# A hybrid attention step on one core: rests of the weights in pieces, the sample's search ended later and with a running count, the last output tile in halves

## Chip, cores and metric

The kernel runs on one core of one Trainium2 chip. The metric is the device time of one execution in microseconds; the median of 3 runs of the kernel before is 369.21 us (368.37 to 370.45).

## What is computed

One inference step of one layer, for a prompt of 512 tokens and a sample of 32 tokens, width 1024, all in float32:

```python
z = _rmsnorm(x, g) @ w_in
oa = _band_prompt(qa, ka, va, rel_bias_a)      # group A: 6 heads x 64, own chunk and 8 before it
ob = _dsa_prompt(qb, kb, vb, qi, ki, wi)       # group B: only the top-k keys of an indexer's scores
om = _attend(qm, mk, mv, None)                 # group M: 4 heads over 256 memory tokens
o = concat([oa * silu(ga), ob * silu(gb), om * silu(gm)])
y = _rmsnorm(x + o @ w_out, g_final)
```

The sample does the same against caches; its group B chooses 256 of 1056 keys per query (`lax.top_k`, which takes the earlier key where two scores are equal). The new keys and values of all groups are outputs too.

## The kernel before

Each float32 product is made of three fp32r products. A weight chunk `raw` is rounded by ScalarE to `wh`; its rest `wl = raw - wh` is made in one subtraction by GpSimd, for chunks 0 and 2 by VectorE (`w_split`, lines 429 to 445). The tokens are split in the same way into `xTh` and `xTl`, and TensorE adds `xTh*wh`, `xTl*wh` and `xTh*wl`. A chunk holds 4, 2 or 3 blocks of 128 rows and 128 to 384 columns.

The Python code is also the planner. `Line` keeps a clock for every engine with its own costs; work beside the projections is written as generators, which wait with `yield` until a time or with `line.wait` until a condition. `line.run` gives out the matmuls of a projection one after the other, and ahead of each it lets every generator run whose time has come (`beside`). The order in which the instructions are given out is the order on each engine, so a different condition or cost at one place reorders the others after it. All instructions are made through helpers, so the profile puts them on one line (L240), and they are known by the tiles that they write and read.

The order of projections is the indexer's (`i`), then `EARLY` (group A, memory, their queries and gates), then `LATE`: `gb0`, `kb`, `qb`, `vb`, `gb1`, `gb2`. Meanwhile the indexer's scores are made, VectorE picks the prompt's keys (`picks`, MAX8 and MATCH_REPLACE8 on `ysel`), and attention units (`attend`) follow one another: scores into two PSUM banks (`bank<-k,q`), VectorE reads them, ScalarE takes the exponent, TensorE turns the result (`ident,z`) and multiplies by the values (`pt,v`), and `finish` multiplies by the gate (`o<-bank,gate`), which frees the bank. There are eight PSUM banks.

Rows of kb and qb pass through `rope` (line 718): two products out of PSUM (`rt`, `kb` or `qb`) and a sum by VectorE or GpSimd. There is one tile `rt`, so the next rope waits for the sum before it.

`sample_rows` (line 470) collects the sample's own rows of each projection (`kaS`, `kbS`, `qbS`, ...), scales them and applies rope. `sample_choice` (line 942) finds the 256th largest score of each sample query: 16 rounds, each two ScalarE passes over 1056 keys, a matmul of one column (`bank<-bf_ok,over`) and some VectorE instructions of one element. Its end finds the exact threshold `t` and then, in six more rounds of the same kind over `rank`, the position `cut` up to which keys equal to `t` are taken. The mask is left in `ysS` for `sample_b`.

At the end `out_part` multiplies by `w_out` in column groups (256 wide for groups A and M, 512 wide for B as two halves in one bank); for each token tile `evict` adds the bank to `xr` and `settle` makes the final norm: Square with a sum on ScalarE, the sum and the power on GpSimd, two halves of the row scaled by VectorE and ScalarE, and the store by SyncE's queue.

Of the kernel before, what the change touches and what calls it, by code (L numbers as in the profile page):

```python
# [9 lines left out]
F32 = mybir.dt.float32  # L10
# [3 lines left out]
ALU = mybir.AluOpType  # L14
# [3 lines left out]
P = 128  # L18
# [251 lines left out]
def hybrid_step(ctx: ExitStack, tc: tile.TileContext, a: dict):  # L270
# [25 lines left out]
    def give(*tiles):  # L296
        free_banks.extend(held.pop(t.tensor.name) for t in tiles)
# [131 lines left out]
    def w_split():  # L429
        at = {}  # L430
        for i in range(len(w_list)):
            far = i >= n_in + 3 and i % 2
            yield from line.wait(lambda: len(raws) > i and (not far or wq))
            pw, n = (rp, 4) if i < 4 else (wq[0], 2) if far else (wp, 3)
            mine = at.setdefault(n, [])
            yield from line.wait(lambda: len(mine) < n or used["done"] > mine[-n])
            mine.append(i)
            raw = raws[i]
            yield max(line.at(raw), pw.free("wl"))
            wh = pw.tile(list(raw.shape), F32R, tag="wh", name="wh", bufs=n)  # L440
            wl = pw.tile(list(raw.shape), F32R, tag="wl", name="wl", bufs=n)
            rounded(wh, raw)
            yield line.at(wh) - 0.2
            tsub(V if i in WV else G, wl, raw, f(wh))
            split.append((wh, wl))
# [24 lines left out]
    def sample_rows(nm, n, p):  # L470
# [14 lines left out]
        give(p)  # L485
        yield from line.wait(lambda: NT in normed)
        yield max(line.at(rs[0:T, NT:NT + 1]), line.at(out) - 0.2)
# [449 lines left out]
    bi = {n: cp.tile([P, 1], I32, name="bi_" + n) for n in ("thr0", "thr1", "flip", "neg", "ok", "dig", "next")}  # L937
    bf = {n: cp.tile([P, 1], F32, name="bf_" + n) for n in ("sum", "t", "c", "m", "need", "cut", "try", "dig", "min")}
    bf["ok"] = cp.tile([P, 1], BF16, name="bf_ok")
    over4 = cp.tile([P, 4, T], BF16, name="over4")  # L940

    def sample_choice():
        flp, neg, ok, dig, nxt = (bi[n] for n in ("flip", "neg", "ok", "dig", "next"))
        thr = bi["thr0"], bi["thr1"]
        s_, t, c, m, need, cut, tr_, digf, okf = (bf[n] for n in ("sum", "t", "c", "m", "need", "cut", "try", "dig", "ok"))
# [4 lines left out]
        V.tensor_copy(digf, dig)  # L950
        G.memset(over4, 0.0)
# [3 lines left out]

        def passed(of, bias, least_, scale=1.0):

            yield line.at(bias)
            A.activation(junkS, of, AF.Sign, bias=bias, accum_out=s_)
            A.activation(okf, s_, AF.Sign, bias=least_, scale=scale)  # L960
# [15 lines left out]
        for b in range(30, -1, -2):  # L976
# [561 lines left out]
    projections(LATE)  # L1538
    line.until(lambda: 1 in gated and all(n in over for n in ("kb", "qb", "vb")))
    rox.close()  # L1540
# [36 lines left out]

    def out_part(parts, c0, n, done, order):

        ws = [w_next(1 + i) for i in range(len(parts))]  # L1580
        for t in order:
            acc, = take(1)
            for i, ((m, k0, nk, p0, pn), (wh, wl)) in enumerate(zip(parts, ws)):
                o = acc[:, p0:p0 + pn]
                yield (wh, wl) + ((acc,) if i == 0 else ()) + ((oS[:, k0:k0 + nk, :],) if t == NT else
                                  tuple(x[:, :, t * P:(t + 1) * P] for x in oT[m]))
                for k in range(nk):
# [6 lines left out]
                    else:  # L1594
# [4 lines left out]
                        PE.matmul(o, hh, wl[:, k, :], start=False, stop=en)  # L1599
            line.spawn(evict([acc], [1], lambda _, p, t=t: residual(t, p, c0, n), lambda t=t: done(t)))  # L1600

# [5 lines left out]
    for c0 in range(0, D, 256):  # L1607
        line.run(out_part(((0, 0, 3, 0, 256), (2, 6, 2, 0, 256)), c0, 256, lambda t: None, (0, 1, 2, 3, NT)))
    line.until(lambda: 1 in over and count["done"] == len(units))
# [8 lines left out]

    def settle(t, c0):
        rows = P if t < NT else T  # L1620
        x = xr[t][:, c0:c0 + 512]
        s_ = ss[:rows, t, :]
        last = c0 + 512 == D
        yield line.at(x) - 0.2
        A.activation(sq[:rows], x, AF.Square, scale=D ** -0.5, accum_out=s_[:, c0 // 512:c0 // 512 + 1])
        if not last:
            G.tensor_tensor(x, x, gf[:rows, c0:c0 + 512], op=ALU.mult)
        yield line.at(s_) - 0.2
        if not last:
            V.tensor_scalar(s_[:, 2:3], s_[:, 0:1], EPS, None, op0=ALU.add)  # L1630
# [12 lines left out]
    while line.tasks:
# [66 lines left out]
```

## Time and profile before

| | us |
|---|---|
| median of 3 runs | 369.21 |
| time of the profiled execution | 369.7 |
| its span (first to last instruction) | 367.9 |
| TensorE busy | 355.6 (97%) |
| VectorE busy | 282.4 (77%) |
| ScalarE busy | 223.0 (61%) |
| GpSimd busy | 176.2 (48%) |

The profile is of one execution. PE is TensorE, PEld its weight loads, DVE VectorE, ACT ScalarE, POOL GpSimd, SP SyncE. A row of the timeline gives start, duration, engine, operation, output and inputs, how many, and in brackets the idle time of the engine ahead of it and what ended it. 1.8 us of the execution lie outside the span.

### The profile page before, as it was taken

To read this page: it belongs to the slowest core of one execution; us is meant where nothing else is said; L and a number is where in the kernel's file an instruction comes from. 1 tells how busy PE (TensorE), PEld (TensorE's weight loads), DVE (VectorE), ACT (ScalarE), POOL (GpSimd) and SP (SyncE) were. 2 spreads that over 40 slices of the span, in tenths; PEclk is the share of its full clock that TensorE was granted. 3 is DMA by queue.
4 is the path that set the end of the run, shared out by engine and by line. 5 is a ranking of instruction groups with operands and counts; after the bars stand their busy time and mean duration, and the time that the engine had idled before them with its cause. 6 is when DMAs were issued, how large, how long until landed. Compare 5 with 4: busy or idle time off the path is not lost.

```text
span 367.9 us, 7969 instructions
## 1 busy us (share of the span) xinstructions
PE 355.6 (97%) x2959; PEld 321.6 (87%) x2959; DVE 282.4 (77%) x731; ACT 223.0 (61%) x524; POOL 176.2 (48%) x202
## 2 busy tenths in 40 slices
PE   8999999999999999999999998999999999999992
PEld 8989679999989988889899787898999879899991
DVE  2682996989999999999999989986764676623553
ACT  5865756997776946788737343767864556311343
POOL 1787953475443834446548447352145206233651
PEclk9999999999999999999999998999999999999998
DMA  7996631366483330611322115121147932120005
GB/s 252 361 361 220 172 116 43 130 178 172 127 272 104 116 89 11 175 47 45 86 64 67 45 48 172 37 59 54 48 159 259 375 98 88 43 102 2 0 20 224
DMA packets 41478, 46.35 MB, mean 126 GB/s; under 512 B 5184, under 2 KB 36544, under 8 KB 41440
## 3 DMA queue, kind: packets, MB, share of 16 engines
q1 hardware_dynamic: 41440, 45.85, 39.2%
q8 instruction: 23, 0.38, 0.4%
q14 instruction: 15, 0.12, 0.1%
HBM read 39.67 MB, written 6.16 MB: 125 GB/s over the span
## 4 chain that ended last, share of the span: by engine, by line
PE 77%; DVE 11%; ACT 3%; POOL 3%; issue 2%; DMA 2%; SPq 1%; POOLq 0%; ACTq 0%; DVEq 0%
PE bank L240 77%; DMA raw<-in_w_in_dram 2%; DVE rt L240 1%; POOL wl L240 1%; DVE rank L240 1%; DVE KSs L240 1%; ACT sq L240 1%; DVE ysel L240 1%; DVE kb L240 1%; POOL ss L240 1%; DVE kbS L240 1%; DVE m L240 1%; SPq L240 1%; DVE bf_m L240 1%; POOL kb L240 1%
## 5 line engine op out<-in xcount | busy, mean ns | idle before, releaser
L240 POOL TENSOR_TENSOR wl<-raw,wh 128x512 fp32r<-128x512 f32 (+2 forms) x68 | 105.1, 1553 | 95.6 <-ACT wh L240 91.8
L240 PE MATMUL bank<-wh,xTh 128*128 128x384 f32 (+1 forms) x192 | 67.5, 351 | 0.1
L240 ACT ACTIVATE wh<-raw 128x512 fp32r<-128x512 f32 (+2 forms) x70 | 49.8, 717 | 28.4 <-issue 11.8
L240 PE MATMUL bank<-wl,xTh 128*128 128x384 f32 (+1 forms) x192 | 64.0, 334 | 0.2 <-DVE wl L240 0.2
L240 PE MATMUL bank<-wh,xTl 128*128 128x384 f32 (+1 forms) x192 | 63.7, 332 | 0.0
L240 ACT ACTIVATE z<-z,st 128x256 f32<-128x256 f32 (+3 forms) x76 | 40.6, 549 | 35.1 <-DVE st L240 35.0
L240 PE MATMUL bank<-xTh,wh 128*128 128x272 f32 x208 | 46.3, 304 | 0.3 <-DVE stS L240 0.3
L240 PE MATMUL bank<-xTh,wl 128*128 128x272 f32 x208 | 43.0, 288 | 0.0
L240 PE MATMUL bank<-xTl,wh 128*128 128x272 f32 x208 | 43.0, 288 | 0.0
L240 PEld LDWEIGHTS bank<-wh,xTh 128*128 128x128 f32 x192 | 36.6, 191 | 3.9 <-issue 2.6
L240 PEld LDWEIGHTS bank<-wl,xTh 128*128 128x128 f32 x192 | 36.5, 190 | 0.6 <-DVE wl L240 0.4
L240 PEld LDWEIGHTS bank<-wh,xTl 128*128 128x128 f32 x192 | 36.8, 191 | 0.3 <-DVE xTl L240 0.3
L240 PEld LDWEIGHTS bank<-xTh,wh 128*128 128x128 f32 x208 | 32.7, 189 | 3.1 <-issue 2.0
L240 PEld LDWEIGHTS bank<-xTl,wh 128*128 128x128 f32 x208 | 32.6, 188 | 0.0
L240 PEld LDWEIGHTS bank<-xTh,wl 128*128 128x128 f32 x208 | 32.5, 189 | 0.0
L240 DVE MAX8 m<-ysel 128x8 f32<-128x256 f32 (+2 forms) x48 | 26.4, 550 | 0.1
L240 DVE MATCH_REPLACE8 ysel<-m,ysel 128x256 f32<-128x256 f32 (+2 forms) x48 | 26.0, 542 | 0.0
L240 PE MATMUL bank<-ident,z 128*128 128x128 f32 (+1 forms) x161 | 25.2, 274 | 0.5 <-ACT z L240 0.4
L240 DVE TENSOR_TENSOR xr<-bank,xr 128x256 f32<-128x256 f32 (+1 forms) x24 | 12.2, 510 | 16.7 <-PE bank L240 15.6
L240 PEld LDWEIGHTS bank<-ident,z 128*128 128x128 f32 (+1 forms) x161 | 18.3, 140 | 3.6 <-issue 1.4
L240 DVE SCALAR_TENSOR_TENSOR ysel<-r,wI,ysel 128x256 f32<-128x256 f32 (+2 forms) x21 | 18.5, 880 | 3.0 <-ACT r L240 2.5
L240 ACT ACTIVATE junkS<-ysS,bi_neg 128x1056 int8<-128x1056 f32 x16 | 18.7, 1172 | 2.3 <-DVE bi_neg L240 2.3
(317 smaller groups left out, 884.1 us busy)
## 6 DMA issues: line engine op xcount, KB each, us to landing
raw<-in_w_in_dram SPq DMA_DIRECT2D x20, 384.0 KB, 3.3
raw<-in_w_in_dram SPq DMA_DIRECT2D x26, 256.0 KB, 2.9
raw<-in_w_out_dram SPq DMA_DIRECT2D x8, 384.0 KB, 3.0
nat<-in_x_prompt_dram SPq DMA_DIRECT2D x4, 512.0 KB, 8.2
raw<-in_w_mem_kv_dram SPq DMA_DIRECT2D x8, 256.0 KB, 2.9
xr<-in_x_prompt_dram SPq DMA_DIRECT2D x4, 512.0 KB, 5.3
out_dram<-xr SPq DMA_DIRECT2D x4, 512.0 KB, 2.6
xr<-in_x_t_dram SPq DMA_DIRECT2D x3, 544.0 KB, 5.9
```

The costliest lines, as they stand in the source:

```text
L240: return fn(*args, **kw)
```

## The change

Five edits, in the order of the code:

1. `w_split`: the rest `wl` is made in two instructions (chunks of 4 or 2 blocks) or three (3 blocks) in place of one.
2. `sample_rows`: the rows kbS and qbS are scaled and turned by rope only when the prompt's qb is finished.
3. `sample_choice`: the end of the search waits for that too. The six rounds for `cut` go; in their place stand a mask of keys equal to `t` (int8), a running count over it (`tensor_tensor_scan`) and one comparison with the number that is still needed.
4. `out_part`: in the last column group the last prompt tile (`apart`) uses two banks, each added to `xr` and squared by itself; `settle` takes pieces of any width.
5. `settle`: the left half of the prompt's third tile is scaled by VectorE in place of ScalarE.

```diff
@@ w_split
-            tsub(V if i in WV else G, wl, raw, f(wh))
+            step = max(raw.shape[1] // 2, 1)
+            for k in range(0, raw.shape[1], step):
+                c = slice(k, k + step)
+                tsub(V if i in WV else G, wl[:, c], raw[:, c], f(wh)[:, c])
@@ sample_rows
-        yield from line.wait(lambda: NT in normed)
+        yield from line.wait(lambda: NT in normed and (nm not in ("kb", "qb") or "qb" in over))
@@ sample_choice
-        yield from line.wait(lambda: count["scored"] >= len(TILES))
+        yield from line.wait(lambda: count["scored"] >= len(TILES) and "qb" in over)
...
         V.tensor_scalar(junkS, ysS, t, None, op0=ALU.is_gt, op1=ALU.add, accum_out=c)
-        V.tensor_scalar(need, c, -2.0, float(2 * TOPK_S - NKS) + 0.5, op0=ALU.mult, op1=ALU.add)
-        G.iota(rank, pattern=[[-1, NKS]], base=2048, channel_multiplier=0, allow_small_or_imprecise_dtypes=True)
-        yield max(line.at(rank), line.idle(V))
-        V.scalar_tensor_tensor(rank, ysS, t, rank, op0=ALU.is_equal, op1=ALU.mult)
-        V.memset(cut, 2048.5)
-        V.tensor_scalar(tr_, digf, 1024.0, cut, op0=ALU.mult, op1=ALU.subtract)
-        for b in range(10, -1, -2):
-            w = float(1 << b)
-            p = yield from passed(rank, tr_, need, -1.0)
-            V.tensor_scalar(m, p[:, 0:1], 0.5 * w, 1.5 * w, op0=ALU.mult, op1=ALU.add)
-            give(p)
-            V.tensor_scalar(cut, m, -1.0, cut, op0=ALU.mult, op1=ALU.add)
-            if b:
-                V.tensor_scalar(tr_, digf, 0.25 * w, cut, op0=ALU.mult, op1=ALU.subtract)
+        V.tensor_scalar(need, c, -1.0, TOPK_S + 0.5, op0=ALU.mult, op1=ALU.add)
+        V.tensor_scalar(junkS, ysS, t, None, op0=ALU.is_equal)
+        yield line.idle(V)
+        V.tensor_tensor_scan(rank, junkS, junkS, 0.0, op0=ALU.add, op1=ALU.max)
+        yield line.idle(V)
+        V.scalar_tensor_tensor(rank, rank, need, junkS, op0=ALU.is_lt, op1=ALU.mult)
         yield line.idle(V)
         V.tensor_scalar(ysS, ysS, t, BIG, op0=ALU.is_le, op1=ALU.mult)
         yield line.idle(V)
-        V.scalar_tensor_tensor(ysS, rank, cut, ysS, op0=ALU.is_le, op1=ALU.mult)
+        V.scalar_tensor_tensor(ysS, rank, 0.5, ysS, op0=ALU.is_lt, op1=ALU.mult)
@@ out_part
+                if i and t in apart:
+                    line.spawn(evict([acc], [1], lambda _, p, t=t: residual(t, p[:, 0:p0], c0, p0),
+                                     lambda t=t: done(t, c0, p0)))
+                    acc, = take(1)
@@ settle
-        A.activation(y[:, 0:512], y[:, 0:512], AF.Copy, scale=s_[:, 4:5])
+        V.scalar_tensor_tensor(y[:rows, 512:D], y[:rows, 512:D], run, gf[:rows, 512:D], op0=ALU.mult, op1=ALU.mult)
+        if t == NT - 2:
+            V.tensor_scalar(y[:rows, 0:512], y[:rows, 0:512], run, None, op0=ALU.mult)
+        else:
+            A.activation(y[:rows, 0:512], y[:rows, 0:512], AF.Copy, scale=run)
```

How this moves the instructions is shown at two places, both on VectorE (DVE). The first is ahead of the first read of group B's scores, `z,st<-bank,mb`, which frees the banks of that unit. ISA stands for the fused add with minimum and for the readout of its accumulator; `bf_` and `bi_` are one-element tiles of the search. Before:

```order
L240 TENSOR_TENSOR vbS<-bank,vbS 32x384 x2
L240 COPY pt<-bank 128x512
L240 TENSOR_TENSOR kl<-bank,k 128x512
L240 TENSOR_SCALAR vbS<-vbS,rs 32x384
L240 SCALAR_TENSOR_TENSOR o<-bank,gate 128x256
L240 COPY pt<-bank 128x512
L240 SCALAR_TENSOR_TENSOR ql<-bank,q 128x512
L240 TENSOR_SCALAR bf_m<-bank 128x1
L240 TENSOR_SCALAR bf_cut<-bf_m,bf_cut 128x1
L240 TENSOR_SCALAR bf_try<-bf_dig,bf_cut 128x1
L240 SCALAR_TENSOR_TENSOR o<-bank,gate 128x256
L240 ISA z,st<-bank,mb_68 128x128
```

With the change:

```order
L240 SCALAR_TENSOR_TENSOR ql<-bank,q 128x512
L240 TENSOR_SCALAR rank<-ysS,bf_t 128x528
L240 ISA rank,bf_try<-rank,ysS 128x528
L240 ISA bf_try 128x1
L240 TENSOR_TENSOR bf_m<-bf_m,bf_try 128x1
L240 TENSOR_SCALAR bf_c<-bf_c 128x1
L240 SCALAR_TENSOR_TENSOR bf_m<-bf_c,bf_m 128x1
L240 TENSOR_TENSOR bf_t<-bf_t,bf_m 128x1
L240 TENSOR_SCALAR junkS,bf_c<-ysS,bf_t 128x1056
L240 TENSOR_SCALAR bf_need<-bf_c 128x1
L240 TENSOR_SCALAR junkS<-ysS,bf_t 128x1056
L240 ISA z,st<-bank,mb_68 128x128
```

The second half of the search for the exact threshold, which stood 91 DVE rows ahead of that read before, now lies between the query's low part (`ql`) and the read of the scores. Ahead of `ql` stand, since the last rope of qb, also the first half of that search, the first count, and the ropes of kbS and qbS.

The second place is the end of the program, from the second prompt tile's sum on (`xr_3894`, `xr_3895`, `xr_3896` are the second, third and fourth prompt tile before; `xr_3910`, `xr_3911`, `xr_3912` the same with the change). Before:

```order
L240 TENSOR_TENSOR xr_3895<-bank,xr_3895 128x512
L240 SCALAR_TENSOR_TENSOR xr_3894<-xr_3894,ss,gf 128x512
L240 TENSOR_TENSOR xr_3896<-bank,xr_3896 128x512
L240 SCALAR_TENSOR_TENSOR xr_3895<-xr_3895,ss,gf 128x512
L240 SCALAR_TENSOR_TENSOR xr_3896<-xr_3896,ss,gf 128x512
```

With the change:

```order
L240 TENSOR_TENSOR xr_3911<-bank,xr_3911 128x512
L240 SCALAR_TENSOR_TENSOR xr_3910<-xr_3910,ss,gf 128x512
L240 TENSOR_TENSOR xr_3912<-bank,xr_3912 128x256 x2
L240 SCALAR_TENSOR_TENSOR xr_3911<-xr_3911,ss,gf 128x512
L240 TENSOR_SCALAR xr_3911<-xr_3911,ss 128x512
L240 TENSOR_SCALAR ss<-ss 128x1
L240 SCALAR_TENSOR_TENSOR xr_3912<-xr_3912,ss,gf 128x512
```

The last tile's sum comes in two pieces, the third tile's left half has moved to DVE, and a one-element sum of the last tile's squares (`ss<-ss`) now stands behind both instructions of the third tile.

## Rows read from the trace of the kernel before

**Rows 1.** The page's part 1: busy us, share of the span, instructions.
```profile
PE 355.6 (97%) x2959; PEld 321.6 (87%) x2959; DVE 282.4 (77%) x731; ACT 223.0 (61%) x524; POOL 176.2 (48%) x202
```
**Rows 2.** Waits of PE: who waited for whom, us, times, longest.
```profile
PE bank L240 <- DVE o L240: 1.3, 1, 1.3
PE bank L240 <- DVE stk L240: 0.7, 2, 0.4
```
**Rows 3.** Timeline around PE's longest wait inside the program.
```profile
220.82 3.93 POOL L240 TENSOR_TENSOR wl<-raw,wh 128x768 fp32r<-128x768 f32 x2
...
221.25 1.83 DVE L240 TENSOR_TENSOR kb<-rt,kb 128x384 f32<-128x384 f32 x1
...
222.48 0.38 PE L240 MATMUL bank<-k,q 64*128 64x256 f32 x1
...
223.69 0.42 DVE L240 SCALAR_TENSOR_TENSOR o<-bank,gate 128x256 f32<-128x256 f32 x1
...
224.17 0.38 PE L240 MATMUL bank<-k,q 64*128 64x256 f32 x1 [1.31 <-DVE o L240]
...
225.08 0.44 PE L240 MATMUL bank<-wh,xTh 128*128 128x384 f32 x1
```
**Rows 4.** Groups of DVE by form: busy us, mean ns.
```profile
L240 DVE TENSOR_TENSOR rt<-bank,sin 128x384 f32<-128x384 f32 x8 | 4.4, 553 | 1.8 <-POOL kb L240 1.1 <-POOL qb L240 0.6
...
L240 DVE TENSOR_SCALAR z<-z,st 128x512 f32<-128x512 f32 x6 | 3.2, 531 | 0.2
...
L240 DVE CUSTOM_DVE_ANT_0 rank<-rank,ysS 128x528 f32<-128x528 f32 x2 | 1.9, 937 | 0.1
...
L240 DVE TENSOR_SCALAR_CACHE_REDUCE junkS<-ysS,bf_t 128x1056 int8<-128x1056 f32 x2 | 2.6, 1310 | 0.0
...
L240 DVE SCALAR_TENSOR_TENSOR ysS<-rank,bf_cut,ysS 128x1056 f32<-128x1056 f32 x1 | 1.3, 1318 | 0.0
...
L240 DVE TENSOR_SCALAR bf_try<-bf_dig,bf_cut 128x1 f32<-128x1 f32 x6 | 1.3, 215 | 0.4
```
**Rows 5.** Windows: length, busy us per engine, PE's granted clock, DMA share, GB/s.
```profile
224.00:229.00 5.00, 4.83 (x25) 4.26 (x27) 4.69 (x13) 2.72 (x5) 3.24 (x3) 0.66 0.98 315
```
**Rows 6.** Groups of POOL by form: busy us, mean ns; idle before.
```profile
L240 POOL TENSOR_TENSOR wl<-raw,wh 128x768 fp32r<-128x768 f32 x28 | 51.9, 1861 | 32.6 <-ACT wh L240 31.8 <-POOL keysB L240 0.5
L240 POOL TENSOR_TENSOR wl<-raw,wh 128x512 fp32r<-128x512 f32 x38 | 50.1, 1324 | 57.3 <-ACT wh L240 54.2 <-PE bank L240 2.9
...
L240 POOL TENSOR_TENSOR kb<-rt,kb 128x384 f32<-128x384 f32 x3 | 3.1, 1018 | 5.3 <-DVE kb L240 5.3
...
L240 POOL TENSOR_TENSOR oMl<-o,oMh 128x256 fp32r<-128x256 f32 x4 | 3.0, 739 | 3.9 <-ACT oMh L240 3.9
```
**Rows 7.** Timeline of PE around one matmul of the search's end.
```profile
241.62 0.34 PE L240 MATMUL bank<-wh,xTl 128*128 128x384 f32 x1
241.80 0.34 PE L240 MATMUL bank<-wl,xTh 128*128 128x384 f32 x1
241.98 0.18 PE L240 MATMUL bank<-bf_ok,over 128*128 128x1 bf16 x1
...
242.28 0.34 PE L240 MATMUL bank<-wh,xTl 128*128 128x384 f32 x1
```
**Rows 8.** Timeline of the end: POOL, DVE and ACT after the last matmuls.
```profile
360.62 0.55 POOL L240 TENSOR_TENSOR ss<-ss,nhalf 128x1 f32<-128x1 f32 x1
360.65 0.69 DVE L240 TENSOR_TENSOR xr<-bank,xr 128x512 f32<-128x512 f32 x1 [0.81 <-PE bank L240]
361.20 0.72 ACT L240 ACTIVATE xr<-xr,ss 128x512 f32<-128x512 f32 x1 [0.94 <-POOL ss L240]
361.26 0.74 DVE L240 SCALAR_TENSOR_TENSOR xr<-xr,ss,gf 128x512 f32<-128x512 f32 x1
361.83 0.61 ACT L240 ACTIVATE sq<-xr 128x512 f32<-128x512 f32 x1
...
362.61 0.19 POOL L240 TENSOR_TENSOR ss<-ss 128x1 f32<-128x1 f32 x1 [1.45 <-ACT sq L240]
```

More of the change, by code (lines that the diff above doesn't have):

```diff
@@ L937, in hybrid_step @@
     bi = {n: cp.tile([P, 1], I32, name="bi_" + n) for n in ("thr0", "thr1", "flip", "neg", "ok", "dig", "next")}
-    bf = {n: cp.tile([P, 1], F32, name="bf_" + n) for n in ("sum", "t", "c", "m", "need", "cut", "try", "dig", "min")}
+    bf = {n: cp.tile([P, 1], F32, name="bf_" + n) for n in ("sum", "t", "c", "m", "need", "try", "min")}
     bf["ok"] = cp.tile([P, 1], BF16, name="bf_ok")
@@ L944, in sample_choice @@
         thr = bi["thr0"], bi["thr1"]
-        s_, t, c, m, need, cut, tr_, digf, okf = (bf[n] for n in ("sum", "t", "c", "m", "need", "cut", "try", "dig", "ok"))
+        s_, t, c, m, need, tr_, okf = (bf[n] for n in ("sum", "t", "c", "m", "need", "try", "ok"))
         G.iota(dig, pattern=[[0, 1]], base=0, channel_multiplier=1)
@@ L949, in sample_choice @@
         V.memset(dig[0:T], 1)
-        V.tensor_copy(digf, dig)
         G.memset(over4, 0.0)
@@ L954, in sample_choice, with passed @@
         V.memset(bf["min"], float(NKS - 2 * TOPK_S) + 0.5)
-        def passed(of, bias, least_, scale=1.0):
+        def passed(of, bias, least_):
             yield line.at(bias)
             A.activation(junkS, of, AF.Sign, bias=bias, accum_out=s_)
-            A.activation(okf, s_, AF.Sign, bias=least_, scale=scale)
+            A.activation(okf, s_, AF.Sign, bias=least_)
             yield line.sure(okf)
@@ L1538, in hybrid_step @@
     projections(LATE)
-    line.until(lambda: 1 in gated and all(n in over for n in ("kb", "qb", "vb")))
+    line.until(lambda: 1 in gated and all(n in over and n in news for n in ("kb", "qb", "vb")))
     rox.close()
@@ L1576, in hybrid_step, with out_part @@
     line.spawn(sample_b())
-    def out_part(parts, c0, n, done, order):
+    def out_part(parts, c0, n, done, order, apart=()):
         ws = [w_next(1 + i) for i in range(len(parts))]
@@ L1599, in out_part @@
                         PE.matmul(o, hh, wl[:, k, :], start=False, stop=en)
-            line.spawn(evict([acc], [1], lambda _, p, t=t: residual(t, p, c0, n), lambda t=t: done(t)))
+            f0 = parts[-1][3] if t in apart else 0
+            line.spawn(evict([acc], [1], lambda _, p, t=t, f0=f0: residual(t, p[:, f0:n], c0 + f0, n - f0),
+                             lambda t=t, f0=f0: done(t, c0 + f0, n - f0)))
     def residual(t, acc, c0, n):
@@ L1607, in hybrid_step @@
     for c0 in range(0, D, 256):
-        line.run(out_part(((0, 0, 3, 0, 256), (2, 6, 2, 0, 256)), c0, 256, lambda t: None, (0, 1, 2, 3, NT)))
+        line.run(out_part(((0, 0, 3, 0, 256), (2, 6, 2, 0, 256)), c0, 256, lambda *_: None, (0, 1, 2, 3, NT)))
     line.until(lambda: 1 in over and count["done"] == len(units))
@@ L1617, in hybrid_step, with settle @@
     ss = fp.tile([P, NT + 1, 8], F32, name="ss")
-    def settle(t, c0):
+    pieces = [0] * (NT + 1)
+    def settle(t, c0, n):
         rows = P if t < NT else T
-        x = xr[t][:, c0:c0 + 512]
+        x = xr[t][:, c0:c0 + n]
         s_ = ss[:rows, t, :]
-        last = c0 + 512 == D
+        j = pieces[t]
+        pieces[t] += 1
+        new, run, old = s_[:, 2 * j:2 * j + 1], s_[:, 2 * j + 1:2 * j + 2], s_[:, 2 * j - 1:2 * j]
         yield line.at(x) - 0.2
[L1625 to L1630, printed above, removed]
+        A.activation(sq[:rows, 0:n], x, AF.Square, scale=D ** -0.5, accum_out=new)
+        if j == 0:
+            G.tensor_tensor(x, x, gf[:rows, c0:c0 + n], op=ALU.mult)
+        yield line.at(new) - 0.2
+        if c0 + n < D:
+            V.tensor_scalar(run, new, EPS if j == 0 else old, None, op0=ALU.add)
@@ L1631, in settle @@
             return
-        G.tensor_tensor(s_[:, 3:4], s_[:, 1:2], s_[:, 2:3], op=ALU.add)
-        G.tensor_tensor(s_[:, 4:5], s_[:, 3:4], nhalf[:rows], op=ALU.pow)
-        yield line.at(s_) - 0.2
+        G.tensor_tensor(run, new, old, op=ALU.add)
+        G.tensor_tensor(run, run, nhalf[:rows], op=ALU.pow)
+        yield line.at(run) - 0.2
         y = xr[t]
-        V.scalar_tensor_tensor(x, x, s_[:, 4:5], gf[:rows, c0:D], op0=ALU.mult, op1=ALU.mult)
-        A.activation(y[:, 0:512], y[:, 0:512], AF.Copy, scale=s_[:, 4:5])
+        V.scalar_tensor_tensor(y[:rows, 512:D], y[:rows, 512:D], run, gf[:rows, 512:D], op0=ALU.mult, op1=ALU.mult)
@@ L1638, in settle @@
+        if t == NT - 2:
+            V.tensor_scalar(y[:rows, 0:512], y[:rows, 0:512], run, None, op0=ALU.mult)
+        else:
+            A.activation(y[:rows, 0:512], y[:rows, 0:512], AF.Copy, scale=run)
         DMA.dma_start(a["y_prompt"][t * P:(t + 1) * P, :] if t < NT else a["y_sample"], y)
     for c0 in range(0, D, 512):
-        line.run(out_part(((1, 3, 3, 0, 256), (1, 3, 3, 256, 256)), c0, 512, lambda t, c0=c0: line.spawn(settle(t, c0)),
-                          (NT, 0, 1, 2, 3)))
+        line.run(out_part(((1, 3, 3, 0, 256), (1, 3, 3, 256, 256)), c0, 512, lambda t, c, n: line.spawn(settle(t, c, n)),
+                          (NT, 0, 1, 2, 3), (NT - 1,) if c0 else ()))
```

## Prediction

> **What bounds the kernel now.** I read the page's busy shares first. TensorE is busy for 355.6 of 367.9 us, 97%; no other engine is above 77% [rows 1]. So the time moves only by what is taken from TensorE's own work, from the few places where it stands still, from its clock, or from the end, where it has nothing left to do. A faster GpSimd or VectorE pays only at such a place. I then asked the waits for these places. There is one wait inside the program of more than half a microsecond: 1.3 us on VectorE's `o`, the gate product that frees a bank [rows 2]. The two on `stk` make 0.7 together [rows 2].
>
> The timeline around the long wait tells why `o` is late. GpSimd makes rests of 128x768, two in 3.93 us [rows 3]. At 221.25, beside them, VectorE's rope sum `kb<-rt,kb` takes 1.83 us [rows 3], where VectorE's other rope instructions of 128x384 take 0.553 [rows 4]. Its `o` starts only at 223.69 and lasts 0.42; TensorE's next scores start at 224.17 after 1.31 us of nothing [rows 3]. From the windows I read what the pause does afterwards: from 224 to 229 the granted clock is 0.66 on the mean, with TensorE busy for 4.83 of 5.00 us [rows 5]. [...] The pause thus cost 1.3 + 1.7 = 3.0 us.
>
> [...]
>
> **The change, part by part**
>
> *A, the stall at 222.8, −3.0.* The planner gives out a new order, in which the scores that waited here stand earlier, and VectorE no longer turns kbS and qbS nor searches for the sample's threshold near them. If the same meeting occurs, a piece of 384 columns holds VectorE for about 1.02 us (GpSimd's sum of that width) in place of 1.86 [rows 6]. I take the whole 3.0; its bounds are 0 (the pause turns up elsewhere) and −3.0.
>
> *B, the six rounds, −0.7.* Each had a one-column matmul on TensorE. From 241.80 to 242.28 there are two steps with it, 0.48 us; without it one step is 241.80 − 241.62 = 0.18 [rows 7], so 0.48 − 0.36 = 0.12 is its price, six times 0.7. As bounds I take 0.08 and 0.2 each, −0.5 to −1.2. The twelve ScalarE passes and the small instructions of VectorE in these rounds lie beside TensorE's work and bring nothing by themselves.
>
> *C, the end, 0.* The last matmul ends near 360.62. Before, the last tile was added to `xr` at 360.65 in 0.69, its Square was held until 361.83 by ScalarE's scaling of the third tile (361.20, 0.72), and GpSimd's sum stood at 362.61 [rows 8]. Halves free the bank sooner and the scaling leaves ScalarE. But the one-element sum of the last tile's squares now stands on VectorE behind both instructions of the third tile. These can't start before GpSimd's power of that tile ends (360.62 + 0.55 = 361.17): 361.26 + 0.74 [rows 8] + 0.53 for the new scaling (a 128x512 product by a column takes 0.531 [rows 4]) is 362.53, and with the sum itself 362.6 to 362.7, where it was 362.61. So nothing; the bound is −0.9 if that sum doesn't wait, +0.1 if it all follows in a row.
>
> *D, the start, −0.4.* The two `stk` waits make 0.7 [rows 2] and follow VectorE instructions that lie beside long rests. Shorter pieces may take half; bounds −0.7 and +0.7.
>
> *E, a new queue ahead of group B's first scores, +0.8.* This is the place that the first order rows show. After the last rope of qb VectorE has, up to the reads that free the bank for the first matmul of `gb1`: two counts 2 × 1.31, two half searches of a compare (0.69, the price of a 128x512 sum [rows 8]) and a custom operation (0.94), so 2 × 1.63; eight scalings and ropes of kbS and qbS at 0.553 at most; `kl` and `ql` at 0.69 each; nine one-element instructions at 0.215; the int8 mask at 1.31 at most [rows 4]; three score reads at 0.42 (as `o` [rows 3]). That is 2.6 + 3.3 + 4.4 + 1.4 + 1.9 + 1.3 + 1.3 = 16.2 us. TensorE has from the end of qb 96 matmuls at 0.175 (16.8), eight transposes (about 0.9) and the 24 score matmuls (2.5 times the columns that took from 224.17 to 225.08 [rows 3], 2.3), in all 20.0 us. VectorE starts later than that, since the four ropes go one by one through one `rt` tile: two products (1.1) and a sum of 1.02 by GpSimd [rows 6] each, 7.0 for the chain, of which 3.2 lie before the end of qb. So TensorE has 20.0 − 3.8 = 16.2. The two are level: no cover is left. Of the eight instructions with two SBUF inputs (six of the ropes, two of the searches) each can meet a GpSimd piece. I take one such meeting, 1.0, less 0.2 for the scalings and the mask, which I priced at their most. Bounds 0 and, with half of them held for 1.02, +4.
>
> *F, GpSimd's pieces, 0.* A rest of 128x512 as two pieces of 256 costs 2 × 0.739 = 1.48 in place of 1.32; 128x768 as two costs 2.04 in place of 1.86, as three of 256 2.2 [rows 6]. Over 66 rests this is 38 × 0.16 + 28 × 0.2 to 0.36, 12 to 16 us more. GpSimd is busy for 48% [rows 1], and stands idle for 32.6 and 57.3 us ahead of these very instructions, waiting for ScalarE's `wh` [rows 6]: that is the cover. Without it a rest comes up to 0.36 us later.
>
> *G, the running count, 0.* No row of before has a scan. The nearest are the one-pass instructions over 1056 columns, 1.31 and 1.32 [rows 4]; I bound it by one and by two of them, 1.3 and 2.6, and take 2.2. The scan, a comparison and a last product stand behind the first score reads, where the six rounds stood before; what is held there is the next pair's `kl` and `ql`, off TensorE's path by the count of E's kind. [...]
>
> *Sum:* −3.0 − 0.7 + 0 − 0.4 + 0.8 = −3.3. The profiled execution took 369.7 (span 367.9 and 1.8 around it), so 366.4; it stood 0.5 above the median, so **365.9**.
>
> **Rivals**
>
> 1. *Slower: E decides.* Seven of the eight two-input instructions meet GpSimd's pieces, which are now twice as many. TensorE then waits 7 × 1.02 = 7.1 us ahead of `gb1` and, as after the pause of 1.31, loses 1.7 to the clock. With E's 0.8 taken out, the other terms give −4.1; −4.1 + 7.1 + 1.7 is +4.7, **373.9**. With the clock's loss the sign turns at a wait of 2.4, and over 0.5% is lost from 4.3. For it: no slack, the single-file queue. Against: most instructions on VectorE beside rests keep their usual time now, the rope of 1.83 is the exception. Chance 0.12.
> 2. *No change: the pause only moves.* Another bank is freed late by a reordered VectorE, for 1.3 us and 1.7 of clock; B and D and E remain: −0.7 − 0.4 + 0.8 = −0.3, **368.9**. For it: a planner with a new order has many such places, and VectorE is at 77%. Chance 0.25.
> 3. *More is gained.* E costs nothing, the `stk` waits go (−0.7), the last sum isn't held (−0.9): −3.0 − 0.7 − 0.9 − 0.7 = −5.3, **363.9**. This is also where the end's edit does what it appears to be for; my forecast says that it does not. Chance 0.14.
>
> My own case has the rest, 0.49, from 364.2 (no wait in E) to 367.3.
>
> **How the numbers follow.** The measurement can tell about 0.5% from no change, 1.85 us: faster means 367.36 or less, slower 371.06 or more. Faster are my own case and rival 3, 0.63; same is rival 2, 0.25; slower is rival 1, 0.12. The range runs from 362.8 (rival 3 with B at its bound of −1.2 and another half microsecond) to 369.6 (rival 2 with D at its bad end, +0.7), and leaves out rival 1 and a little of both ends, under 0.2.
>
> **What would show it.** A: no wait of TensorE over 1 us on VectorE's `o`, and no stretch of 5 us with a granted clock near 0.66. B: the one-column matmuls fall from 22 to 16. C: GpSimd's last sum about 2.0 us after the last matmul; at 1.2 it is rival 3. D: `stk` below 0.7. E: a wait ahead of the first `gb1` matmul on VectorE's `st`, under 1 us in my case, over 2.4 in rival 1. F: no more than some tenths of waits on `wl`. G: the scan at 1.3 to 2.6 us. The forecast is wrong if the pause, with its clock, is still there in another place, or if the wait in E passes 3 us.

## The result and the profile after

The changed kernel takes 366.24 us (median of 20 runs, 365.49 to 369.11); the kernel before took 369.48 beside it (20 runs). The ratio is 0.9922, with a 95% interval from 0.9908 to 0.9935. The forecast of 365.9 lies close to it, but only in part for its own reasons: as the sections below show, its term E was too kind, its term A counted a loss of the clock that only some runs have, and a gain of about 1.6 us was in no term at all.

The page's busy shares of the changed kernel, in the form of [rows 1]:

```profile
PE 351.2 (96%) x2953; PEld 318.6 (87%) x2953; DVE 270.8 (74%) x710; ACT 216.7 (59%) x514; POOL 197.4 (54%) x278
```

TensorE is still the bound. It is busy for 4.4 us less; GpSimd has 76 instructions and 21.2 us more, of which little is seen on TensorE (its waits on `wl`, the rests that GpSimd makes, are 0.2). TensorE's waits in the changed kernel, which answer to [rows 2]:

```profile
PE bank L240 <- DVE ql L240: 1.6, 1, 1.6
...
PE bank L240 <- ACT wh L240: 0.5, 1, 0.5
PE bank L240 <- DVE st L240: 0.4, 1, 0.4
PE bank L240 <- DVE gate L240: 0.4, 1, 0.4
...
PE bank L240 <- POOL wl L240: 0.2, 1, 0.2
```

The wait on `o` of 1.3 us is gone, and so are the two on `stk`. In their place stands one of 1.6 on `ql`, with 0.4 on `st` behind it. Apart from one of 1.4 on `nhalf` at the start, which both kernels have, the listed waits add up to 3.3 us before and 4.0 after: in sum TensorE does not wait less. The windows around the new wait (length, busy us of the engines, granted clock, DMA share, GB/s), beside [rows 5]:

```profile
252.00:254.00 2.00, 0.36 (x5) 0.20 (x4) 1.97 (x5) 0.58 (x1) 0.76 (x1) 1.00 0.56 166
254.00:259.00 5.00, 4.56 (x35) 3.79 (x35) 4.79 (x20) 0.80 (x5) 0.00 (x0) 1.00 0.19 63
```

The granted clock is 1.00 after this pause of 1.6 us, though it is longer than the one of 1.3 before, after which its mean was 0.66 [rows 5]. Why `ql` is late is seen in the timeline of VectorE from the last ropes of qb on:

```profile
241.00 0.55 DVE L240 TENSOR_TENSOR qb<-bank,cos 128x384 f32<-128x384 f32 x1
241.46 0.14 DVE L240 TENSOR_SCALAR bf_t<-bi_thr 128x1 f32<-128x1 f32 x1
241.64 1.01 DVE L240 SCALAR_TENSOR_TENSOR bf_m<-bf_t 128x1 f32<-128x1 f32 x1
242.69 0.94 DVE L240 SCALAR_TENSOR_TENSOR bf_t<-bf_m,bf_t 128x1 f32<-128x1 f32 x1
243.66 1.32 DVE L240 TENSOR_SCALAR_CACHE_REDUCE junkS<-ysS,bf_t 128x1056 int8<-128x1056 f32 x1
...
244.90 0.87 DVE L240 TENSOR_SCALAR kbS<-kbS,rs 32x384 f32<-32x384 f32 x1
245.88 1.18 DVE L240 TENSOR_TENSOR rt<-kbS,sin64S 32x384 f32<-32x384 f32 x1
247.10 0.98 DVE L240 TENSOR_TENSOR kbS<-kbS,cos64S 32x384 f32<-32x384 f32 x1
248.11 0.98 DVE L240 TENSOR_TENSOR kbS<-rt,kbS 32x384 f32<-32x384 f32 x1
249.02 0.40 DVE L240 TENSOR_SCALAR qbS<-qbS,rs 32x384 f32<-32x384 f32 x1
249.45 0.55 DVE L240 TENSOR_TENSOR rt<-qbS,sin64S 32x384 f32<-32x384 f32 x1
...
252.20 1.12 DVE L240 CUSTOM_DVE_ANT_0 rank<-rank,ysS 128x528 f32<-128x528 f32 x1
253.25 0.68 DVE L240 SCALAR_TENSOR_TENSOR ql<-bank,q 128x512 fp32r<-128x512 f32 x1
```

and in GpSimd's timeline beside it:

```profile
241.62 1.01 POOL L240 TENSOR_TENSOR qb<-rt,qb 128x384 f32<-128x384 f32 x1 [1.14 <-DVE bf_t L240]
242.59 6.09 POOL L240 TENSOR_TENSOR wl<-raw,wh 128x384 fp32r<-128x384 f32 x6
```

While GpSimd works through its rope sum and six pieces in a row, six of the VectorE instructions shown from 241.64 to 248.11, which read SBUF alone, each take about as long as one piece (6.09 / 6 = 1.02): one-element ones 1.01 and 0.94, the rows of kbS 0.87 to 1.18. The count at 243.66 does not: its 1.32 is what it takes in [rows 4]. As soon as the pieces end, at 248.7, the same instructions on qbS take 0.40 and 0.55. I call an instruction that is made longer in this way held, and each such case a meeting. The six held rows add up to 5.96 us; at 0.16, 0.16, 0.40 and three times 0.55 they would be 2.37, so 3.6 us of them are holding. The custom operation at 252.20, beside the next two pieces, is a seventh: 1.12, where the same at 254.37 takes 0.71. In all 4.0 us of VectorE's queue ahead of `ql` are holding.

The end of the program, beside [rows 8], from GpSimd and VectorE:

```profile
357.13 0.55 POOL L240 TENSOR_TENSOR ss<-ss,nhalf 128x1 f32<-128x1 f32 x1
...
357.71 0.75 DVE L240 SCALAR_TENSOR_TENSOR xr<-xr,ss,gf 128x512 f32<-128x512 f32 x1 [0.60 <-POOL ss L240]
358.38 0.48 DVE L240 TENSOR_SCALAR xr<-xr,ss 128x512 f32<-128x512 f32 x1
358.78 0.21 DVE L240 TENSOR_SCALAR ss<-ss 128x1 f32<-128x1 f32 x1
...
359.13 0.19 POOL L240 TENSOR_TENSOR ss<-ss 128x1 f32<-128x1 f32 x1 [1.45 <-DVE ss L240]
```

The last matmul ends at 356.66, so GpSimd's last sum starts 2.47 us after it; before it was 1.99. It waits for VectorE's one-element `ss`, which stands behind the two products of the third tile, as the second order of the change shows.

One more difference is in no wait. At the end of the output projection the matmuls follow each other without a gap in both kernels. The two ends of the last 24 steps, of the kernel before:

```profile
357.46 0.28 PE L240 MATMUL bank<-wl,oBh 128*128 128x256 f32 x1
...
360.34 0.28 PE L240 MATMUL bank<-wl,oBh 128*128 128x256 f32 x1
```

and of the changed kernel:

```profile
353.66 0.28 PE L240 MATMUL bank<-wl,oBh 128*128 128x256 f32 x1
...
356.38 0.28 PE L240 MATMUL bank<-wl,oBh 128*128 128x256 f32 x1
```

24 steps, from start to start, take 2.88 us before (120 ns each) and 2.72 after (113 ns), with a granted clock of 1.00 in both. The output projection has 384 matmuls of this width, so about 2.5 us. The instructions are the same; the tiles are not where they were. The change drops two one-element tiles (`cut` and `dig`), each of which takes 32 bytes of each partition, and the tiles allocated behind them move down by 64 bytes: the addresses of `wh` and `wl`, and of `xTh` and `xTl`, go from 96 to 32 modulo 128. The attention outputs that `wh` and `wl` are multiplied with, `oAh`, `oBh` and `oMh`, stay at 96.

### The profile page after: what moved, and what is told of

It is laid out like the page before. It is cut to its first block, busy times and chain, and to the rows that moved or that the text cites. A ratio compares the mean times of both kernels' runs of the same rounds, so it can differ in the third digit from the quotient of the medians.

```text
span 364.4 us, 8024 instructions
## 1 busy us (share of the span) xinstructions
PE 351.2 (96%) x2953; PEld 318.6 (87%) x2953; DVE 270.8 (74%) x710; ACT 216.7 (59%) x514; POOL 197.4 (54%) x278
## 4 chain that ended last, share of the span: by engine, by line
PE 65%; DVE 26%; issue 2%; POOL 2%; DMA 2%; ACT 1%; SPq 1%; POOLq 0%; DVEq 0%; ACTq 0%
PE bank L240 65%; DVE z L240 4%; DVE ysel L240 3%; DVE m L240 3%; DVE gate L240 2%; DMA raw<-in_w_in_dram 2%; DVE st L240 2%; DVE rank L240 2%; DVE kbS L240 1%; DVE rt L240 1%; DVE junkS L240 1%; DVE qbS L240 1%; DVE vbS L240 1%; POOL ss L240 1%; DVE qb L240 1%
## 5 line engine op out<-in xcount | busy, mean ns | idle before, releaser
L240 POOL TENSOR_TENSOR wl<-raw,wh 128x256 fp32r<-128x256 f32 (+2 forms) x144 | 125.8, 900 | 91.6 <-ACT wh L240 83.6
L240 PE MATMUL bank<-wh,xTh 128*128 128x384 f32 (+1 forms) x192 | 65.9, 343 | 0.5 <-ACT wh L240 0.5
L240 ACT ACTIVATE z<-z,st 128x256 f32<-128x256 f32 (+3 forms) x71 | 37.7, 546 | 29.8 <-DVE st L240 29.8
L240 PE MATMUL bank<-xTh,wh 128*128 128x272 f32 x208 | 47.2, 308 | 0.4 <-DVE st L240 0.4
L240 ACT COPY pt<-bank 128x512 f32<-128x512 f32 (+1 forms) x29 | 15.6, 541 | 13.2 <-PE bank L240 13.0
```

The costliest lines, as they stand in the source:

```text
L240: return fn(*args, **kw)
```

## Experiments

Each is compared with runs of the kernel before on the same chip, whose medians were 369.0 to 369.7. Ratios are to these.

### Where the weights lie

```diff
e1, the changed kernel
-    bf = {... ("sum", "t", "c", "m", "need", "try", "min")}
+    bf = {... ("sum", "t", "c", "m", "need", "try", "min", "pad0", "pad1")}
e2, the kernel before
-    bf = {... ("sum", "t", "c", "m", "need", "cut", "try", "dig", "min")}
+    bf = {... ("sum", "t", "c", "m", "try", "min")}
+    bf3 = cp.tile([P, 3], F32, name="bf_3")
+    bf["need"], bf["cut"], bf["dig"] = bf3[:, 0:1], bf3[:, 1:2], bf3[:, 2:3]
```

> The changed kernel with two unused one-element tiles, each of which takes 32 bytes of a partition: every instruction keeps its place on its engine, and the weights' tiles (wh, wl) return to the addresses of the kernel before, 64 bytes higher. Theory (place): in the output projection TensorE starts a 256-wide matmul every 120 ns in the kernel before and every 113 to 114 ns in the changed one, because the change freed two small tiles and so moved the weights by 64 bytes; the step goes back to 120 ns, the last matmul starts about 2.4 us later, and the time is 368.4 to 368.9. Rival (run): the step differs from one execution to the next, or hangs on the order of the instructions; it stays at 113 to 114 and the time at 366.0 to 366.6.

> The kernel before with three one-element tiles of the search (need, cut, dig) put into one tile of three columns, so that the weights' tiles lie 64 bytes lower, at the addresses of the changed kernel; the order of the instructions is that of the kernel before. Theory (place): the 256-wide matmuls of the output projection go from 120 to 113 or 114 ns a step, and the time from 369.5 to 367.0 (366.7 to 367.4) with nothing else of the change. Rival (run): 120 ns and 369.2 to 369.8.

e1 took 368.06 us (ratio 0.9966, 0.9953 to 0.9980), e2 367.73 (0.9963, 0.9946 to 0.9980; the kernel before had 369.23). The ends of the last 24 steps in e1:

```profile
355.93 0.28 PE L240 MATMUL bank<-wl,oBh 128*128 128x256 f32 x1
...
358.81 0.28 PE L240 MATMUL bank<-wl,oBh 128*128 128x256 f32 x1
```

and in e2:

```profile
353.87 0.28 PE L240 MATMUL bank<-wl,oBh 128*128 128x256 f32 x1
...
356.59 0.28 PE L240 MATMUL bank<-wl,oBh 128*128 128x256 f32 x1
```

The step is 120 ns in e1 and 113 in e2: it goes with the addresses, in both directions, with the order of the instructions unchanged. In time it is +1.8 us (366.24 to 368.06) and −1.5 us (369.23 to 367.73), less than the 2.5 that the steps make and less than was expected. So about half of the change's gain is the place of the weights, a side effect of two dropped tiles. With the tiles where they were, the five edits gain 1.2 us (e1 beside its own runs of the kernel before, 369.23 to 368.06).

Part of what is missing is seen at the end. GpSimd's last sum in e1 and in e2:

```profile
361.10 0.19 POOL L240 TENSOR_TENSOR ss<-ss 128x1 f32<-128x1 f32 x1 [1.45 <-DVE ss L240]
```

```profile
359.32 0.19 POOL L240 TENSOR_TENSOR ss<-ss 128x1 f32<-128x1 f32 x1 [1.44 <-ACT sq L240]
```

The last matmul ends at 359.09 in e1 and at 356.87 in e2, so the sum stands 2.01 and 2.45 us after it; in the kernel before it was 1.99, in the changed one 2.47. It goes with TensorE's step, not with the edits at the end: GpSimd's last sums follow each other at 2.27 us a tile in the kernel before (360.34 and 362.61) and in the changed one (356.86 and 359.13) alike, while a tile's 18 matmuls take 2.16 or 2.04. The faster TensorE runs further ahead of the chain of Square, sum, power and scaling, and 0.4 to 0.5 of its gain is lost there.

e2 also tells something of the pause, which it still has, and of the windows after it:

```profile
223.95 0.38 PE L240 MATMUL bank<-k,q 64*128 64x256 f32 x1 [1.27 <-DVE o L240]
```

```profile
224.00:229.00 5.00, 5.00 (x40) 4.49 (x41) 4.69 (x12) 2.65 (x5) 3.04 (x3) 1.00 0.96 306
```

The same pause, 1.27 us, and a clock of 1.00 behind it. The 0.66 of [rows 5] does not follow from the pause alone.

The single runs of the kernel before show how much that counts. Of the 59 that were taken beside e1 to e12, 30 have a mean granted clock of 0.994 or more and a median of 368.9 us; the other 29 have a lower one and a median of 370.0. The lower clock goes with 1.1 us, in about half of the runs. Where in these runs the clock was low is not recorded, so that it is the stretch behind the pause is likely and not shown.

What counts about the place is open in part. In e5 the token tiles moved too, so that they differ from the weights modulo 128 bytes, on top of e3 (below):

```diff
     xp = pool(xpx, "xp", "left")
+    xp.tile([P, 16], F32, name="xpad")
```

> The kernel of e3 with 64 unused bytes ahead of xTh and xTl, so that in the projections the weights and the token tiles no longer start at the same place of a 128-byte line; the order of the instructions is that of e3. Theory (pair): what counts in e1 and e2 is not where the weights lie but whether the moving and the stationary operand start at the same place modulo 128 bytes (in the kernel before wh and oAh both at 96: 120 ns; in the changed one 32 and 96: 113 ns; mTh with wh the other way round, 113 at the best against 116). Then the 480 matmuls of 384 columns go from 176 ns by 6 to 7 ns down, 3 us, and the time is 362.4 to 363.2. Rival (only the weights' own place, or only widths of 256): 365.4 to 365.9, with 176 ns.

It took 365.14 us (0.9899, 0.9871 to 0.9928), half a microsecond below e3, with intervals that overlap. In the groups by form the mean duration of the 160 `wh,xTh` matmuls falls from 352 to 349 ns, the others by 1. The expected 3 us did not come. Whether it is the two operands' places relative to each other, as I supposed, or something narrower that holds for 256 columns, is not settled.

### The end

```diff
-            V.tensor_scalar(run, new, EPS if j == 0 else old, None, op0=ALU.add)
+            if j == 0:
+                V.tensor_scalar(run, new, EPS, None, op0=ALU.add)
+            else:
+                G.tensor_tensor(run, new, old, op=ALU.add)
```

> The changed kernel, with the running sum of the last tile's squares made by GpSimd instead of VectorE; one instruction changes its engine, nothing else moves. Theory: that one-element sum, held on VectorE behind the two instructions of the third tile, sets the end; GpSimd's last sum then starts about 1.25 us after the last matmul's end instead of 2.47, VectorE's last product about 1.0 earlier (it must still finish the third tile's two), and the time is 365.1 to 365.5. Rival (the stores or the third tile's products end last anyway): 366.0 to 366.4.

It took 365.64 us (0.9925, 0.9897 to 0.9953). By the median it is 0.6 less than the changed kernel; the two ratios do not tell them apart. The trace shows the step (last matmul's end at 356.40):

```profile
357.74 0.51 POOL L240 TENSOR_TENSOR ss<-ss 128x1 f32<-128x1 f32 x1 [0.17 <-ACT sq L240]
358.32 0.68 POOL L240 TENSOR_TENSOR ss<-ss,nhalf 128x1 f32<-128x1 f32 x1
```

```profile
358.11 0.48 DVE L240 TENSOR_SCALAR xr<-xr,ss 128x512 f32<-128x512 f32 x1
359.03 0.75 DVE L240 SCALAR_TENSOR_TENSOR xr<-xr,ss,gf 128x512 f32<-128x512 f32 x1 [0.44 <-POOL ss L240]
```

GpSimd's last sum starts 1.34 us after the last matmul in place of 2.47, and VectorE's last product 2.63 in place of 3.32. GpSimd's two one-element instructions take 0.51 and 0.68 where the same stood at 0.19 and 0.55, beside VectorE's two products of the third tile. So in the trace 0.7 of the expected 1.0 arrives.

### The pieces, and the postponement

e7 is the kernel before with the first edit alone, e8 the changed kernel without it, e4 the changed kernel with the search free to start as before:

```diff
e4
-        yield from line.wait(lambda: count["scored"] >= len(TILES) and "qb" in over)
+        yield from line.wait(lambda: count["scored"] >= len(TILES))
```

> The kernel before with the weights' rests in pieces, and nothing else of the change; the weights lie where they lay. Theory (A by the pieces): shorter pieces let VectorE's rope sum through, the pause of 1.31 near 222 and the waits on stk go: 367.0 to 368.6. Rival (the pieces are worth nothing, VectorE meets more pieces for as long in sum; what A won came from the order): 368.8 to 370.5.

> The changed kernel with each rest made in one instruction again. Theory (A by the pieces): VectorE's two-input instructions are held for up to 1.9 us by GpSimd, and the queue ahead of group B's first scores, already short of time, gets longer: 367.0 to 369.5, with the waits on ql and st longer than 2.1 in all. Rival (pieces are worth nothing): 365.6 to 366.8, GpSimd busy some 14 us less.

> The changed kernel with the end of the sample's search no longer waiting for the finish of qb; kbS and qbS still wait. Theory: the search stands in VectorE's queue ahead of ql and of the first score reads (about 7 us of it), and the waits of TensorE on ql (1.64) and st (0.44) come from that; without it both go and the time falls by about 2, to 364.0 to 364.8. Rival (the queue is as long without the search, or the search now holds another bank): 365.8 to 367.0, with a wait of over 1 us in another place.

e7 took 374.63 us (1.0138, 1.0116 to 1.0160): the kernel before with the pieces alone is slower. The pause on `o` and the waits on `stk` are gone, as the theory had it, but there is a larger one:

```profile
PE bank L240 <- DVE kb L240: 6.5, 3, 5.4
```

and VectorE's timeline ahead of it:

```profile
215.09 1.42 DVE L240 CUSTOM_DVE_ANT_0 rank<-rank,ysS 128x528 f32<-128x528 f32 x1
...
216.55 0.82 DVE L240 TENSOR_TENSOR bf_m<-bf_m,bf_try 128x1 f32<-128x1 f32 x1
```

With more instructions on GpSimd the planner gives out another order and puts the search between the ropes of kb, where TensorE waits for their banks. e4, 372.72 us (1.0108, 1.0084 to 1.0132), has the same:

```profile
PE bank L240 <- DVE kb L240: 4.7, 2, 3.4
PE bank L240 <- DVE ql L240: 2.0, 1, 2.0
```

So my theories on e7 and e4 fell: the search alone is not what holds `ql` (it waits 2.0 without it), and the postponement is needed once the rests are in pieces; without it the change would be slower than before. e8, without the pieces, took 367.88 us (0.9956, 0.9938 to 0.9975), 1.6 more than the changed kernel, with waits on `ql` of 2.5 in all and on `stk` of 0.7: here the pieces, with the order that goes with them, are worth something, as the first theory had it. GpSimd is busy for 179.7 us in e8, so 17.7 of its 21.2 more are the pieces.

The `stk` waits by themselves are no clean sign of the pieces, since e2, with whole rests, has none either. From 12 to 80 us TensorE stands still for 1.1 to 1.2 us in the kernel before, e8 and e12 (below), all with whole rests, for 0.5 in e2, and for 0 to 0.3 in the changed kernel, e1, e3, e7, e9 and e10, which have pieces.

### What holds ql

> The kernel of e3 with the end of the search put behind the first reads of group B's scores (it waits for qb and for one scored unit of group B); the ropes of kbS and qbS stay. Theory (E): the waits of TensorE on ql (1.6) and st (0.4) come from the search in VectorE's queue; both go, the search lies between later reads, where z is needed later, and the time is 363.6 to 364.4. Rival (the queue only moves: the next unit's ql and kl come later instead, or z): 365.2 to 366.5 with a wait of over 1 us on z, pt or ql near 260.

> The kernel of e3 with the scalings and ropes of kbS and qbS put off until one unit of group B is scored; the search stays where the change put it. Theory (E by the ropes): in the changed kernel these eight instructions take 0.4 to 1.35 each because VectorE and GpSimd alternate, one piece of a rest for one rope instruction; without them kl, ql and the search start 4 to 8 us earlier, the wait on ql (1.6) goes, and the time is 363.6 to 364.6. Rival (E by the search): ql still waits over 1 us, or the first reads of the scores wait as long behind the ropes, 365.2 to 366.2.

> The kernel of e3 with kl and ql first, then the scalings and ropes of kbS and qbS, then the first reads of group B's scores, and the end of the search only after these. Theory (E by the length of the whole queue): neither ql nor the first st waits over 0.5 us, the search lies between later units, where VectorE was busy for 18 of 20 us, and the time is 363.4 to 364.4. Rival (VectorE has no room there either): a wait of over 1 us on z, pt, ql or o between 258 and 285, 365.2 to 367.

```diff
e6, on e3
-        yield from line.wait(lambda: count["scored"] >= len(TILES) and "qb" in over)
+        yield from line.wait(lambda: "qb" in over and count["scored"] > n_am)
e9, on e3
-        yield from line.wait(lambda: NT in normed and (nm not in ("kb", "qb") or "qb" in over))
+        yield from line.wait(lambda: NT in normed and (nm not in ("kb", "qb") or count["scored"] > n_am))
e10: as e9, and the search waits for the finished kbS and qbS
```

e6 puts the search behind the first reads of the scores. It took 365.49 us (0.9889, 0.9868 to 0.9910), against 365.64 of e3. TensorE waits on the same `ql` for 2.43 us (the view names `bf_t`, VectorE's next instruction; `ql` ends at 251.21), since the six pieces now meet other rows:

```profile
242.40 1.35 DVE L240 TENSOR_TENSOR rt<-kbS,sin64S 32x384 f32<-32x384 f32 x1 [0.92 <-POOL qb L240]
243.79 1.24 DVE L240 TENSOR_TENSOR kbS<-kbS,cos64S 32x384 f32<-32x384 f32 x1
245.07 1.25 DVE L240 TENSOR_TENSOR kbS<-rt,kbS 32x384 f32<-32x384 f32 x1
246.25 1.17 DVE L240 TENSOR_SCALAR qbS<-qbS,rs 32x384 f32<-32x384 f32 x1
247.45 0.98 DVE L240 TENSOR_TENSOR rt<-qbS,sin64S 32x384 f32<-32x384 f32 x1
```

And the clock falls behind this pause:

```profile
251.26 0.33 PE L240 MATMUL bank<-k,ql 64*128 64x128 f32 x2 [2.43 <-DVE bf_t L240]
...
253.06 0.52 PE L240 MATMUL bank<-wh,xTl 128*128 128x384 f32 x1
253.38 0.52 PE L240 MATMUL bank<-wl,xTh 128*128 128x384 f32 x1
```

The step of these matmuls is 0.32 us where it is 0.175 ahead of the pause; from 251.3 to 256.3 the mean granted clock is 0.66, so by (1 − 0.66) × 5.00, an estimate, another 1.7 us. So e6 does not tell what the later search is worth without that loss.

e9 leaves the search and takes the ropes away. It took 363.77 us (0.9837, 0.9814 to 0.9859), 1.9 less than e3. In its trace the ropes come at 253, where GpSimd has no piece:

```profile
252.89 0.40 DVE L240 TENSOR_SCALAR kbS<-kbS,rs 32x384 f32<-32x384 f32 x1
253.40 0.55 DVE L240 TENSOR_TENSOR rt<-kbS,sin64S 32x384 f32<-32x384 f32 x1
```

`ql` is waited for 0.7. The wait on `st`, 0.8, comes later, at 260.24, right behind the scan, which in this order lies between the first score reads (257.52 to 259.80). e10 took 364.18 us (0.9865, 0.9831 to 0.9899), no wait on `ql` or `st`, but 2.0 on `wl` (longest 1.4, near 275), where the search's last rows, from 272 to 278, lie beside GpSimd's gate products and rests. So neither the search nor the ropes hold `ql` alone: e4 has no search ahead of it and waits 2.0, e9 has no ropes there and waits 0.7, and e10, with neither, waits on it no more.

The holding is not what differs most. In sum it is 4.0 us in the changed kernel, 3.8 in e6 and 3.2 in e9, where the search's rows are held instead (1.01, 0.94, 1.32, 1.12 and 0.84 where they take 0.16, 0.16, 0.48, 0.71 and 0.48). In e12 (below), with whole rests, three meetings (1.02, 1.76 and 1.41) make 3.4. What differs more is how much stands in VectorE's queue between the last rope of qb and `ql`: 11.8 us in e3 (241.21 to 253.01), 8.7 in e9 (241.45 to 250.19). The moment at which TensorE asks moves too: in e6 it comes 3.3 us earlier than in e3 (248.8, 252.1). Of the 1.5 us between the two profiled executions of e3 and e9, 0.8 is less standing of TensorE, the rest less busy time, which I did not follow.

Two more on top of e9:

> The kernel of e9 with the 64 unused bytes of e5; the order of the instructions is that of e9. Theory: the half microsecond of e5 (384-wide matmuls with wh moving 178 and 175 ns, then 173) is a matter of addresses and adds to e9's gain: 363.1 to 363.5. Rival (e5's gain was chance): 363.6 to 364.0.

> The kernel of e9 with each rest in one instruction. Theory (the pieces' worth lies in how long VectorE is held at one meeting): the waits on stk (0.7) return and ql waits longer, as in e8 against the changed kernel: 365.0 to 366.0. Rival (once the ropes are out of the queue the pieces are worth nothing): 363.3 to 364.2.

e11, with the 64 bytes of e5, took 363.19 us (0.9842, 0.9822 to 0.9861). By the median it is 0.6 below e9, by the ratio level with it: inconclusive. e12, without the pieces, took 364.72 (0.9889, 0.9868 to 0.9911), 1.0 more than e9, with 0.8 on `stk` and 1.2 on `ql`; by the ratios half a per cent more. So e9 and e11 beat both kernels, by 1.6% and 0.8%.

## Why the prediction was right, and where it was not

The time, its range and its sign held. The sum behind it did not: with the tiles at their old addresses the five edits gain 1.2 us (e1), where I had summed 3.3, and the other 1.5 to 1.8 came from a term that I did not have. That 365.9 lies so near is in good part luck: two of my terms were too kind by about as much as the missing one brought.

- **A, −3.0:** in the two profiles this is right: the pause of 1.3 is gone and so is the low clock behind it. But e2 shows the same pause without the low clock, and the single runs of before set the lower clock at 1.1 us in half of them, not at 1.7 in all. The 1.7 is (1 − 0.66) × 5.00 us [rows 5], an estimate; microsecond by microsecond the granted clock from 224 to 229 is 1.00, 0.80, 0.50, 0.50 and 0.50. I took one execution's clock for the kernel's. And the pause was less removed than moved: the 1.6 on `ql` is longer than the 1.3 that went. That is the mechanism of rival 2 without its loss of the clock; I had it down as a rival, not as something that A and E bring together.
- **B, −0.7:** the one-column matmuls fall from 22 to 16. Their own price was not tried alone.
- **C, 0:** right, and for the reason given: at equal place of the weights the last sum stands 1.99 us after the last matmul with the old end and 2.01 with the new one (before and e1), 2.45 and 2.47 (e2 and the changed kernel). It waits for the one-element sum behind the third tile's two products, and the trace of e3 shows that 0.7 was to be had there; the ratio of its runs does not confirm it.
- **D, −0.4:** the `stk` waits went (−0.7). They return in e8 and e12, without the pieces; e2, which has whole rests and no `stk` waits, says that not all of it is the pieces. Small new waits on `wh`, `gate` and others came, 0.3 to 0.5 each.
- **E, +0.8:** the mechanism and the place were right, the size was 2.0 (1.6 and 0.4). I counted one meeting with GpSimd; there were seven ahead of `ql` alone, two of them on one-element instructions and one on a scaling with a single input, which I had not counted as able to meet anything. That the first late thing would be `st` was wrong as well: it was `ql`, one step earlier in the same queue. The error was larger than it looks: from 241.46 to the end of the third score read, at 258.71, VectorE's queue takes 17.3 us where I priced 16.2, but 4.0 of it are holding, so I had priced the rows themselves some 3 us too dear (the mask takes 0.76 and not 1.31, the custom operation 0.71 and not 0.94, the scalings 0.40). Rival 1 had the mechanism and set it at seven meetings, the right number though not on the rows that it named. Its price of 7.1 took each at a full 1.02, where they made 4.0 together, and these became 2.0 of waiting.
- **F, 0:** right; the pieces cost GpSimd 17.7 us (e8), not 12 to 16, and were all but hidden.
- **G:** the scan took 2.92 us in the changed kernel, beyond my upper bound of 2.6, and 2.34 in e9:

```profile
L240 DVE TENSOR_TENSOR_SCAN rank<-junkS 128x1056 f32<-128x1056 int8 x1 | 2.3, 2342 | 0.0
```

  In the changed kernel it starts at 261.16 beside a GpSimd rest (261.13), so the 2.92 hold a meeting. It was hidden but for a wait of 0.3 on `z` right behind it (264.84); in e9 TensorE waits 0.8 on `st` behind it. So a price of nothing was a little too kind. The 2.34 is 1.8 times the 1.31 of one pass over as many columns [rows 4].
- **Missed:** the weights' place, −1.5 to −1.8 (e1, e2), 2.5 on TensorE, of which the end gives 0.4 to 0.5 back. No row of before could show it; a look at the addresses of both kernels would have shown that something moved, though not what it is worth.
- **The range:** rival 2 with D at its bad end is −0.7 + 0.7 + 0.8 = +0.8, so 370.0 and not 369.6; and the lower end of my own case, 364.2, needs B and D at their bounds besides no wait in E, which alone gives 365.1.

Together: the place of the weights made about half of the gain and covered E, which cost 1.2 more than I had set. The other half, the 1.2 us of e1, is what was left of A, B, D and E; with waits of 3.3 us in its trace as in the kernel before, it should come from the rounds and the clock, which is argued and not shown. The time was forecast well, the sum was not.

The meetings told against the change more than I let them. The kernel before has one in its longest pause: the rope sum of 1.83 us beside two rests of 3.93 together [rows 3]. With a run of six pieces this happened at one VectorE instruction after the other: the rows at 241.64 to 248.11 take 0.87 to 1.18 us beside pieces of 1.02, all but the count at 243.66, whose 1.32 is its usual time (1.31 [rows 4]). That an instruction needs two SBUF inputs to be held, as my counting in E and in rival 1 took it, was not shown: the scaling at 244.90, with one input besides its column of factors, took 0.87 where the one of qbS took 0.40, and in e9 the compare at 245.50, with one input besides the threshold, took 1.32 where it takes 0.48.

## What to carry to other kernels

Splitting GpSimd's long instructions lowered the price of one meeting here and raised their number, from three in e12 to five in e9; in sum the holding ahead of `ql` stayed about the same (3.2 us in e9, 3.4 in e12). Count the instructions of the other engine that stand beside the whole run of pieces, one-element ones too, and move those that nobody waits for out of the queue ahead of the one that is waited for (e9). When a change frees or adds even small tiles, compare the tiles' addresses before its gain is put down to the edits, and hold the addresses by unused tiles where parts of it are tried one by one. Take the clock's loss after a pause from several executions, not from one.

## What was not expected of the hardware

- The step of TensorE's 256-column matmuls in the output projection is 120 ns or 113 ns by the place of the weights' tiles, 64 bytes apart (before and e1 against after and e2), with no wait and the same instructions, and with a granted clock of 1.00 in the windows of before and after. Over 384 matmuls that is 2.5 us on TensorE, and 1.5 to 1.8 in the medians. Why the place counts is open.
- A pause of 1.3 us was followed by a mean granted clock of 0.66 over 5 us in one execution (before) and of 1.00 in another with the same order (e2), one of 1.6 by 1.00 (the changed kernel) and one of 2.4 by 0.66 (e6).
- One-element instructions of VectorE take 0.94 to 1.01 us beside GpSimd's rope sum and pieces, and 0.16 elsewhere (the changed kernel and e9); GpSimd's own sum of one element took 0.51 beside a VectorE product in e3, where it takes 0.19 in the changed kernel.
